# A state-space input product: one stacked float32r product in place of a plain float32 one

## The chip, the core and the metric

The kernel runs on one core of a Trainium2 chip. The metric is the device time of one execution in microseconds (us). Five engines work in it, each through its own instructions in a fixed order: TensorE (PE: matrix products; its weight loads are listed as PEld), VectorE (DVE), ScalarE (ACT), GpSimd (POOL) and SyncE (SP). SP and POOL also issue the transfers (DMA) between memory and the on-chip buffers.

## What is computed

Two blocks of a network over 256 tokens of 2048 features: a feed-forward part, then a mixer of a state-space half and an attention half, another feed-forward part, and a second block. The change lies in the state-space half. Each group of 16 channels drives 64 complex states; the input to the states is a small product per group:

```python
def s5_mixer(u, log_dt, a_re, a_im, b_re, b_im, c_re, c_im, d, w_glu, b_glu):
    ...
    bu_re = jnp.einsum('bsgh,gph->sbgp', u32, bb_re)
    bu_im = jnp.einsum('bsgh,gph->sbgp', u32, bb_im)
    ...
    _, _, s_re, s_im = lax.associative_scan(_ssm_combine, (a_re_t, a_im_t, bu_re, bu_im), axis=0)
    y = (jnp.einsum('sbgp,ghp->bsgh', s_re, c_re.astype(f32))
         - jnp.einsum('sbgp,ghp->bsgh', s_im, c_im.astype(f32))
         + d.astype(f32) * u32)
```

## The kernel before

**Big products.** All large products go through `gemm` (line 220). Weights are loaded by SP in pieces `raw` (three buffers), ACT rounds half a piece (a unit) to a first float32r part `whi` (line 100), and DVE makes the rest `wlo` (line 110), up to three units ahead of their use. Activations are held in two parts too (`xTh`, `xTl`). A product then is three: hi hi, hi lo, lo hi (lines 240 to 242 with 512 columns, "form B"; lines 248 to 250 with 256 columns, "form T"), accumulated in PSUM tiles `acc`. One unit is 12 products of form B or 24 of form T.

**Side work and its order.** After each unit `tick` (line 194) runs deferred closures and steps side tasks: Python generators that emit a few instructions and then yield the DVE time that they have used, or a pair of that and a number of ticks to wait. `K.finish(task)` (line 212) emits all that is left of a task at that place, with no product in between. Nothing reorders what was emitted: each engine takes its instructions in that order.

**The early chain.** `block1` spawns one chain of side tasks, `early`, under the first feed-forward part: constants, `mod_vectors`, `ctx_norm`, `ssm_prep` (tables of the states), and `mod_rows` (line 518). The last one sums, for two rows and in four halves of 16 pieces of `w_mod`, `macc += mraw * cs` on DVE (line 543: 32 instructions a half, `mraw` loaded by SP through line 534), and then turns each sum by transposes on PE (`mp`, line 553: 16 a half) and reduces them on DVE (line 554). Behind the feed-forward part stands `K.finish(*early)`, and then the input product of the mixer, form T, whose first 1024 columns become `uT` (line 955).

**The state-space part.** `ssm_states` (line 632) is a side task in 16 steps `jp` of two 32-channel groups `j`. `fetch` loads ahead, by POOL's queue, the input matrix `sB`, the output matrix `sC` and the rotation table `rot`. For each group, PE makes `bu` (line 673): two plain float32 products with 32 rows of contraction and 256 columns, straight from `uT`. DVE rotates (`ssw`, `sst`, lines 675 to 681), scans (686) and rotates back (688 to 692), POOL adds (694, 695), and PE multiplies by `sC` (`sy`, line 656). It runs under the mixer's input product and the context's products. `mid` (`m4`) is a pool of ten 4 KB buffers that most of these tiles share.

Of the kernel before, what the change touches and what calls it, by code (L numbers as in the profile page):

```python
# [16 lines left out]
P = 128  # L17
# [6 lines left out]
class Nul:  # L24
    """Stands for every object of the dry pass, which only lists the weight pieces in their order."""
# [17 lines left out]
class Parts(tuple):  # L43
    """The two parts of a k-tile; two: those of it and the next one together."""


class Stream:
    """Weights come in pieces [128, nk, w] (one load each) and are split exactly into two float32r
    parts, half a piece at a time, ahead of the products."""
# [40 lines left out]
    def round(self, upto):  # L90
        """The first parts of the units."""
        K = self.K
        while self.nh < min(upto, len(self.units)):
            p, u, nu, w = self.units[self.nh]
            if u == 0:
                self.load(p + self.RAW)
                self.raw.pop(p - 2, None)
            raw = self.raw[p][:, u * w:u * w + nu * w]
            hi = K.wpool.tile([P, 1024], F32R, tag="whi", name="whi", bufs=self.HI + 1)
            K.nc.scalar.activation(hi[:, :nu * w], raw, AF.Copy)  # L100
            self.parts[self.nh] = hi, raw, nu * w
            self.nh += 1

    def split(self, upto):
        """The second parts of the units."""
# [18 lines left out]
class Core:  # L124
# [22 lines left out]
    # -- tiles -----------------------------------------------------------------  # L147
    def b8(self, name, shape=(P, 2048), dt=F32):
        """A tile of the 8 KB class."""
        return self.big.tile(list(shape), dt, tag="b8", name=name)  # L150

    def m4(self, name, shape=(P, 1024), dt=F32):
        """A tile of the 4 KB class."""
        return self.mid.tile(list(shape), dt, tag="m4", name=name)

    def t1(self, name, shape=(P, 256), dt=F32):
        """A tile of the 1 KB class."""
        return self.sm.tile(list(shape), dt, tag="t1", name=name, bufs=6)

    def t2(self, name, shape=(P, 514), dt=F32):  # L160
        """A tile of the 2 KB class."""
# [11 lines left out]
    # -- order -----------------------------------------------------------------  # L173
# [8 lines left out]
    def step(self, task):  # L182
        """One step of a side task; it yields the vector engine's load of it or (load, ticks to wait)."""
# [21 lines left out]
    def flush(self):  # L205
        """Everything that was deferred, now."""
# [12 lines left out]
    # -- products --------------------------------------------------------------  # L219
    def gemm(self, form, name, kts, n0, w, xT, evac, early=False):  # L220
        """form 'B': tokens on partitions, acc[:, tt, :w]. form 'T': columns on partitions,
        acc[:, nt // 2, (nt % 2) * 256:][:256]. xT[kt]: the two parts [128, 256] of x transposed.
        early: the first pieces are small."""
# [31 lines left out]
    def new_xT(self, n=16, name="xT"):  # L255
        """Room for n k-tiles of a transposed operand in both parts."""
# [9 lines left out]
    def to_xT(self, src, kts, xT, gain=None):  # L266
        """Transposes src(kt, tt) [128 tokens, 128 features] into xT, times gain(kt) [128, 1]."""
# [24 lines left out]
    def rsqrt(self, x, shape, name):  # L292
        """1 / sqrt(x) of a small tile, to full precision: a first guess from the bits, then Newton."""
# [17 lines left out]
class Norm:  # L311
    """Mean square of a token's features, gathered chunk by chunk; then 1 / rms."""
# [21 lines left out]
def ffn(K, w, xT, rstd, h, finished, before_last=None):  # L334
    """h += 0.5 * (silu(x gate) * (x up)) down; finished(n) when the columns n of h are final."""
# [64 lines left out]
def exp_exact(K, x, shape, name, out):  # L400
    """exp of a small tile to float32's precision."""
# [15 lines left out]
def ssm_prep(K):  # L417
    """The state's decay, its angle in turns, and c times (lambda - 1) / a; then the rotation tables."""
# [64 lines left out]
    # cos and -sin of the angle at every token, two states' tiles at a time  # L483
# [22 lines left out]

def mod_vectors(K):
# [10 lines left out]
def mod_rows(K, rows, thirds):  # L518
    """silu(c) w_mod + b_mod of rows: shift and 1 + scale with features on partitions, gate as a row."""
# [48 lines left out]
def layer_stats(K, x, name):  # L568
    """mean and 1 / std of [128, 2048] rows."""
# [25 lines left out]
def token_row(K, r, name):  # L595
    """A value per token (tokens on partitions, [128, 2]) as a row on all partitions [128, 256]."""
# [9 lines left out]
class TokenSquares:  # L606
    """Sum over features of squares, for values with features on partitions."""
# [24 lines left out]
def ssm_states(K, uT):  # L632
    """y, before the gelu and then after it, in the place of u, channels on partitions; its parts to yT."""
    nc, v, a = K.nc, K.nc.vector, K.a
    B, C, E = {}, {}, {}

    def fetch(jp):
        if jp >= 16:
            return
        if jp % 2 == 0:  # L640
            kt = jp // 2
            B[kt] = K.t1("sB", (P, 2, 128))
            nc.gpsimd.dma_start(B[kt][:], a["s_b"][kt])
            C[kt] = K.t1("sC", (P, 2, 4, 32))
            for i in range(2):
                nc.gpsimd.dma_start(C[kt][:, i], K.cfold[i, :, 4 * kt:4 * kt + 4, :])
        E[jp] = K.m4("rot", (P, 2, 2, 256))
# [16 lines left out]
    for jp in range(16):  # L664
        kt, half = divmod(jp, 2)
# [3 lines left out]
        for j in range(2):  # L669
            b = K.ps("bu", (P, 2, 256))  # L670
            q = 32 * (2 * half + j)
            for ri in range(2):
                nc.tensor.matmul(b[:, ri], B[kt][q:q + 32, ri], uT[q:q + 32, kt, :], start=ri == 0, stop=True,  # L673
                                 skip_group_check=True)
# [19 lines left out]
        nc.gpsimd.tensor_add(t[:, 0], t[:, 0], w[:, 0])  # L694
        nc.gpsimd.tensor_sub(w[:, 1], w[:, 1], t[:, 1])
        del E[jp]
        last = jp, t[:, 0], w[:, 1]
# [6 lines left out]
def ssm_gelu(K, uT, yT):  # L704
    """gelu in place, and its two parts."""
# [10 lines left out]
def attend1(K, qT, kT, vt, mix, sq):  # L716
    """Heads by pairs; the three dilated branches as one softmax: mask = 8 log(times a key is seen)."""
# [65 lines left out]
def conv(K, acc, kts, y, scale):  # L783
    """Three taps along the tokens and silu, features on partitions: y[:, n] from the columns' tile kts[n]."""
# [17 lines left out]
def ctx_columns(K, xT):  # L802
    """The columns of block 2's input product that the context feeds: k, v, gates, k and v of the attention."""
# [40 lines left out]
def ctx_values(K, xT):  # L844
    """The context's values of the attention: work for the time in which block 2's input is normed."""
# [11 lines left out]
def ctx_again(K, xT):  # L857
    """The context's operand from memory into both parts."""
# [14 lines left out]
def next_norm(K, h, gain, name, xT, R, spill=None):  # L873
    """What follows each final chunk of h: its part of the rms and its transposes, into xT."""
# [36 lines left out]
def block1(K):  # L911
# [24 lines left out]
    early = [K.spawn(chain(constants1(K), mod_vectors(K), ctx_norm(K), ssm_prep(K), mod_rows(K, (0, 1), (0, 1))))]  # L936

    # ---- ffn 1, and the next norm as its columns become final
# [6 lines left out]
    # ---- the input product: u first, then q, k, v  # L945
# [12 lines left out]

    for dst, n0 in ((uT, 3072), (qT, 0), (kT, 1024)):
        for i in range(2):  # L960
            K.gemm("T", "w_in", kx, n0 + 512 * i, 512, xT2, keepT(dst, i))
# [39 lines left out]
    # ---- the context's part of block 2's input product, under which the mixers run  # L1001
# [56 lines left out]
    # ---- the ssm's half of the output product, then ffn 2  # L1058
# [10 lines left out]
def affine(K, p, kt, row, dst):  # L1069
    """x (1 + scale) + shift of two k-tiles [128, 512], features on partitions, into both parts."""  # L1070
# [14 lines left out]
def log_sigmoid(K, x, sh, out):  # L1085
    """min(x, 0) - log1p(exp(-|x|)); the log by the odd series of (y - 1) / (y + 1). A generator."""
# [17 lines left out]
def gate_rows(K, raw, m0):  # L1104
    """From the gates' columns [128, 2, 32]: b (sums of log f), a = i - b and M = max(m0, running max of a),
    heads on partitions, [8, dir, 256]; dir 1 runs back in time. A generator; leaves K.gr = (b, a, M)."""
# [35 lines left out]
def rows_to_cols(K, rows, name):  # L1142
    """[8, dir, 256] to tokens on partitions [128, t, dir, 8]."""
# [11 lines left out]
def ctx_post(K):  # L1155
    """The context's final state of both mLSTMs, and its keys for the attention."""
# [66 lines left out]
def head_rms(K, x, name):  # L1223
    """1 / rms of 4 heads of 128: x [128, 2, 512] to [128, 8] (t, head)."""
# [9 lines left out]
def rope(K, x, cs, out):  # L1234
    """out = x * cos + turned x * sin, with the norm's weights in the tables cs = (cos, sin) [128, 2, 128]."""
# [639 lines left out]
```

## Time and profile before

| | us |
|---|---|
| median of three runs | 3209.63 |
| lowest, highest | 3209.04, 3209.82 |
| profiled execution, span | 3209.2 |
| PE busy | 3182.3 (99%) |
| DVE busy | 2249.9 (70%) |
| ACT busy | 1484.6 (46%) |
| POOL busy | 264.6 (8%) |

The profile is one execution. A busy share is an average over stages; what a stage costs is read from the order in time. A float32 product of `bu` shows as two records, a float32r one as one. "x8" in a row of the timeline is eight records merged, with the time from the start of the first to the end of the last; since products are pipelined, what one costs on PE is the distance from its start to the next one's.

### The profile page before, as it was taken

Reading aid. Unit: us, or ns where it says so; the run is one execution under the profiler, and the core shown is the slowest. Engines: PE = TensorE matmul, PEld = TensorE weight load, DVE = VectorE, ACT = ScalarE, POOL = GpSimd, SP = SyncE. Lnnn points to the kernel's source line nnn. Section 1 sums busy time; section 2 is a strip of 40 time slices with the busy share of each in tenths; the row PEclk is TensorE's granted clock in tenths of the full one; section 3 lists DMA queues with packets and bytes.
Section 4 is the critical chain, followed back from the end, with each engine's and each line's share of the span. In section 5 each row is a group of like instructions: output and inputs, shape, how many; then the busy total and the mean of one; then the engine's idle time right before and its main releaser. Section 6 shows DMA issues by size and latency. Waiting matters only on the chain.

```text
span 3209.2 us, 41935 instructions
## 1 busy us (share of the span) xinstructions
PE 3182.3 (99%) x16088; PEld 2686.5 (84%) x16088; DVE 2249.9 (70%) x3224; ACT 1484.6 (46%) x1939; POOL 264.6 (8%) x411
## 2 busy tenths in 40 slices
PE   8999999999999999999999999999999999999998
PEld 7888888889978788888888888889988888888887
DVE  6768798786987886764766546767656875445667
ACT  5574444444346445544444444545544444444442
POOL 1000000000231221001000000000001110000001
PEclk9999999999999999999999999999999999999999
DMA  7678677775564555556766556554445555655653
GB/s 266 242 266 289 237 269 263 264 257 201 191 223 159 178 210 203 198 192 207 293 248 241 204 187 220 219 197 171 144 161 175 181 184 205 225 194 186 231 215 132
DMA packets 117146, 684.32 MB, mean 213 GB/s; under 512 B 15612, under 2 KB 15900, under 8 KB 52172
## 3 DMA queue, kind: packets, MB, share of 16 engines
q1 hardware_dynamic: 95616, 610.90, 53.2%
q0 software_dynamic: 21328, 70.74, 6.4%
q8 instruction: 126, 2.06, 0.3%
q14 instruction: 76, 0.61, 0.1%
HBM read 646.41 MB, written 35.18 MB: 212 GB/s over the span
## 4 chain that ended last, share of the span: by engine, by line
PE 97%; DVE 1%; DMA 1%; issue 0%; POOL 0%; ACT 0%; DVEq 0%; SPq 0%; POOLq 0%; ACTq 0%
PE acc L240 27%; PE acc L242 26%; PE acc L241 26%; PE acc L248 3%; PE acc L249 3%; PE acc L250 3%; PE tr L275 1%; PE mN L1429 1%; PE o2p L1343 1%; PE bu L673 1%; PE s L1321 1%; PE sy L656 0%; PE pt L1333 0%; PE ap L726 0%; PE cp L1208 0%
## 5 line engine op out<-in xcount | busy, mean ns | idle before, releaser
L110 DVE TENSOR_TENSOR wlo<-raw,whi 128x1024 fp32r<-128x1024 f32 (+3 forms) x1088 | 1300.2, 1205 | 508.7 <-PE acc L241 411.1
L100 ACT ACTIVATE whi<-raw 128x1024 fp32r<-128x1024 f32 (+3 forms) x1088 | 1115.5, 1031 | 1151.1 <-PE acc L242 920.2
L240 PE MATMUL acc<-whi,xTh 128*128 128x512 f32 (+1 forms) x1472 | 570.9, 388 | 1.9 <-ACT whi L100 1.7
L241 PE MATMUL acc<-wlo,xTh 128*128 128x512 f32 (+1 forms) x1472 | 567.8, 386 | 1.0 <-DVE wlo L110 1.0
L242 PE MATMUL acc<-whi,xTl 128*128 128x512 f32 (+1 forms) x1472 | 567.6, 386 | 0.3 <-DVE xTl L290 0.3
L240 PE MATMUL acc<-whi,uT2h 128*128 128x512 f32 (+2 forms) x992 | 387.5, 391 | 0.0
L242 PE MATMUL acc<-whi,uT2l 128*128 128x512 f32 (+2 forms) x992 | 380.9, 384 | 0.0
L241 PE MATMUL acc<-wlo,uT2h 128*128 128x512 f32 (+2 forms) x992 | 380.3, 383 | 0.0
L240 PEld LDWEIGHTS acc<-whi,xTh 128*128 128x128 f32 x1472 | 277.1, 188 | 58.2 <-issue 2.6
L241 PEld LDWEIGHTS acc<-wlo,xTh 128*128 128x128 f32 x1472 | 277.1, 188 | 53.0 <-DVE wlo L110 2.0
L242 PEld LDWEIGHTS acc<-whi,xTl 128*128 128x128 f32 x1472 | 276.9, 188 | 53.1 <-DVE xTl L290 0.6
L240 PE MATMUL acc<-whi,gTh 128*128 128x512 f32 x688 | 269.5, 392 | 0.5 <-DVE h L375 0.5
L242 PE MATMUL acc<-whi,gTl 128*128 128x512 f32 x688 | 268.3, 390 | 0.0
L241 PE MATMUL acc<-wlo,gTh 128*128 128x512 f32 x688 | 268.1, 390 | 0.0
L240 PEld LDWEIGHTS acc<-whi,uT2h 128*128 128x128 f32 x992 | 186.6, 188 | 37.2 <-issue 2.5
L242 PEld LDWEIGHTS acc<-whi,uT2l 128*128 128x128 f32 x992 | 186.5, 188 | 36.8
L241 PEld LDWEIGHTS acc<-wlo,uT2h 128*128 128x128 f32 x992 | 186.7, 188 | 35.2
L543 DVE SCALAR_TENSOR_TENSOR macc<-mraw,cs,macc 128x1024 f32<-128x1024 f32 x160 | 204.6, 1279 | 3.6 <-DMA mraw<-w_mod 3.6
L240 PE MATMUL acc<-whi,wTh 128*128 128x512 f32 (+1 forms) x416 | 157.2, 378 | 0.0
L241 PE MATMUL acc<-wlo,wTh 128*128 128x512 f32 (+1 forms) x416 | 155.5, 374 | 1.2 <-DVE wlo L110 1.2
L242 PE MATMUL acc<-whi,wTl 128*128 128x512 f32 (+1 forms) x416 | 155.4, 374 | 0.0
L240 PEld LDWEIGHTS acc<-whi,gTh 128*128 128x128 f32 x688 | 129.3, 188 | 27.0 <-ACT whi L100 0.9
(538 smaller groups left out, 4393.1 us busy)
## 6 DMA issues: line engine op xcount, KB each, us to landing
raw<-w_w_in SPq DMA_DIRECT2D x192, 1024.0 KB, 4.9
raw<-w_ffn_w_gate SPq DMA_DIRECT2D x80, 1024.0 KB, 4.9
raw<-w_ffn_w_up SPq DMA_DIRECT2D x80, 1024.0 KB, 4.9
raw<-w_ffn_w_down SPq DMA_DIRECT2D x80, 1024.0 KB, 4.9
mraw<-w_mod SPq DMA_DIRECT2D x96, 512.0 KB, 6.2
raw<-w_w_out SPq DMA_DIRECT2D x28, 1024.0 KB, 4.8
rot<-rot POOLq DMA_DIRECT2D x32, 512.0 KB, 5.0
raw<-w_w_branch_b SPq DMA_DIRECT2D x16, 1024.0 KB, 4.9
```

Source lines behind the costliest of these rows:

```text
L100: K.nc.scalar.activation(hi[:, :nu * w], raw, AF.Copy)
L110: K.nc.vector.tensor_sub(lo[:, :n], raw, hi[:, :n].bitcast(F32))
L240: nc.tensor.matmul(o, xh[:, ts], wh, start=first, stop=False)
L241: nc.tensor.matmul(o, xh[:, ts], wl, start=False, stop=False)
L242: nc.tensor.matmul(o, xl[:, ts], wh, start=False, stop=last)
L248: nc.tensor.matmul(o, wh[:, ns], xh, start=first and n % 2 == 0, stop=False, **sk)
L249: nc.tensor.matmul(o, wh[:, ns], xl, start=False, stop=False, **sk)
L250: nc.tensor.matmul(o, wl[:, ns], xh, start=False, stop=last, **sk)
L275: nc.tensor.transpose(p[:, o:o + 128], src(kt, t), self.ident[:])
L543: v.scalar_tensor_tensor(accs[row][:], w[:], K.cs[:, row, kt:kt + 1], accs[row][:], op0=OP.mult, op1=OP.add)
L673: nc.tensor.matmul(b[:, ri], B[kt][q:q + 32, ri], uT[q:q + 32, kt, :], start=ri == 0, stop=True, skip_group_check=True)
L1321: nc.tensor.matmul(p[:], l[:, t * 128:t * 128 + 128], kk[:, r], start=i == 0, stop=i == 2)
```

## The change

Both operands of `bu` come in two float32r parts, stacked along the contraction: `u` as hi, hi, lo (the first 32 rows, the next 32, the last 32), the input matrix as hi, lo, hi. So one product with 96 rows replaces the float32 one with 32. The parts are made beforehand and go through memory:

- a new side task `ssm_inputs_prep` stands in the early chain ahead of `ssm_prep`: eight times it loads a 96x1024 piece of the (host-side tripled) matrix, rounds it on ACT, subtracts on DVE and stores it to `bst`; its yields are `0, 3`, `0, 1` and `1200`;
- after each half of `uT`, ACT and DVE make `uh` and `ul`, and POOL's queue stores both to `ust`;
- `fetch` loads, in place of one `sB` for two steps, for each step three pieces of `ust` and one of `bst` into a tile `us`;
- POOL's addition writes to `w[:, 0]` and no longer to `t[:, 0]`.

```diff
+def ssm_inputs_prep(K):
+    nc, v = K.nc, K.nc.vector
+    K.bst = K.dram.tile([96, 8192], F32R, name="bst")
+    for c in range(8):
+        cs = slice(c * 1024, c * 1024 + 1024)
+        x, z = K.m4("bx", (96, 1024)), K.m4("bz", (96, 1024), F32R)
+        nc.gpsimd.dma_start(x[:], K.a["s_b"][:, cs])
+        yield 0, 3
+        nc.scalar.activation(z[:], x[:], AF.Copy)
+        yield 0, 1
+        v.tensor_sub(z[32:64], x[32:64], z[32:64].bitcast(F32))
+        nc.gpsimd.dma_start(K.bst[:, cs], z[:])
+        yield 1200
...
-            B[kt] = K.t1("sB", (P, 2, 128))
-            nc.gpsimd.dma_start(B[kt][:], a["s_b"][kt])
...
+        U[jp] = K.m4("us", (96, 2, 512), F32R)
+        for i in range(3):
+            nc.gpsimd.dma_start(U[jp][32 * i:32 * i + 32, 0].rearrange("r (j t) -> r j t", j=2),
+                                K.ust[i // 2, jp // 2, jp % 2].rearrange("j r t -> r j t"))
+        nc.gpsimd.dma_start(U[jp][:, 1], K.bst[:, jp * 512:jp * 512 + 512])
...
-            q = 32 * (2 * half + j)
             for ri in range(2):
-                nc.tensor.matmul(b[:, ri], B[kt][q:q + 32, ri], uT[q:q + 32, kt, :], start=ri == 0, stop=True,
-                                 skip_group_check=True)
+                o = (2 * j + ri) * 128
+                nc.tensor.matmul(b[:, ri], U[jp][:, 1, o:o + 128], U[jp][:, 0, j * 256:j * 256 + 256], start=ri == 0,
+                                 stop=True, skip_group_check=True)
...
-        nc.gpsimd.tensor_add(t[:, 0], t[:, 0], w[:, 0])
+        nc.gpsimd.tensor_add(w[:, 0], t[:, 0], w[:, 0])
...
-        last = jp, t[:, 0], w[:, 1]
+        last = jp, w[:, 0], w[:, 1]
...
-    early = [K.spawn(chain(constants1(K), mod_vectors(K), ctx_norm(K), ssm_prep(K), mod_rows(K, (0, 1), (0, 1))))]
+    early = [K.spawn(chain(constants1(K), mod_vectors(K), ctx_norm(K), ssm_inputs_prep(K), ssm_prep(K), mod_rows(K, (0, 1), (0, 1))))]
...
+        def parts():
+            ks = slice(4 * i, 4 * i + 4)
+            hi, lo = (K.m4(n, (P, 4, 256), F32R) for n in ("uh", "ul"))
+            nc.scalar.activation(hi[:], uT[:, ks], AF.Copy)
+            v.tensor_sub(lo[:], uT[:, ks], hi[:].bitcast(F32))
+            for x, z in enumerate((hi, lo)):
+                nc.gpsimd.dma_start(K.ust[x, ks].rearrange("k a j r t -> (a j r) k t"), z[:])
...
-            K.gemm("T", "w_in", kx, n0 + 512 * i, 512, xT2, keepT(dst, i))
+            K.gemm("T", "w_in", kx, n0 + 512 * i, 512, xT2, keep_u(i) if dst is uT else keepT(dst, i))
```

The order of the instructions shows what this moves. Lines of the changed kernel differ from those of the kernel before: the sums are line 559 there (543 before), the transposes 569 (553), the reductions 570 (554).

PE, where the first feed-forward part (products with `gT`) ends and the mixer's input product (with `xT`) begins; `mp` are the transposes of `mod_rows`. Before:

```order
L240 MATMUL acc<-whi,gTh 128x512
L241 MATMUL acc<-wlo,gTh 128x512
L242 MATMUL acc<-whi,gTl 128x512
L248 MATMUL acc<-xTh,whi 128x256
L249 MATMUL acc<-xTl,whi 128x256
L250 MATMUL acc<-xTh,wlo 128x256
```

After:

```order
L241 MATMUL acc<-wlo,gTh 128x512
L242 MATMUL acc<-whi,gTl 128x512
L569 MATMUL mp<-ident,macc 128x128 x16
L248 MATMUL acc<-xTh,whi 128x256
L249 MATMUL acc<-xTl,whi 128x256
L250 MATMUL acc<-xTh,wlo 128x256
```

The last 16 transposes of the early chain, which before stood in two groups of eight, five and four units (60 and 48 products) ahead of this border, now stand on it.

DVE at the same border: `h` is the last sum of the feed-forward part, `n2` the norm behind it, `macc` the sums of `mod_rows`. Before, from the last transposes of `h` on:

```order
L290 SCALAR_TENSOR_TENSOR xTl<-tr,gains,xTh 128x256 x4
L110 TENSOR_TENSOR wlo<-raw,whi 128x1024 x2
L375 SCALAR_TENSOR_TENSOR h_83<-acc,h_83 128x512
L375 SCALAR_TENSOR_TENSOR h_84<-acc,h_84 128x512
L325 TENSOR_REDUCE n2ms<-n2ss 128x2
```

After:

```order
L290 SCALAR_TENSOR_TENSOR xTl<-tr,gains,xTh 128x256 x4
L559 SCALAR_TENSOR_TENSOR macc<-mraw,cs,macc 128x1024
L110 TENSOR_TENSOR wlo<-raw,whi 128x1024
L559 SCALAR_TENSOR_TENSOR macc<-mraw,cs,macc 128x1024
L110 TENSOR_TENSOR wlo<-raw,whi 128x1024
L559 SCALAR_TENSOR_TENSOR macc<-mraw,cs,macc 128x1024
L375 SCALAR_TENSOR_TENSOR h_83<-acc,h_83 128x512
L375 SCALAR_TENSOR_TENSOR h_84<-acc,h_84 128x512
L325 TENSOR_REDUCE n2ms<-n2ss 128x2
```

and, behind the norm's small steps,

```order
L301 TENSOR_TENSOR n2rt<-n2ry 128x2
L302 SCALAR_TENSOR_TENSOR n2rt<-n2rt,n2ms 128x2
L303 SCALAR_TENSOR_TENSOR n2ry<-n2rt,n2ry 128x2
L559 SCALAR_TENSOR_TENSOR macc<-mraw,cs,macc 128x1024 x29
L570 TENSOR_REDUCE modT<-mp 128x4 x2
L573 TENSOR_SCALAR modT<-modT 128x8
```

Three sums of the last half of `mod_rows` now stand ahead of the last `h`, and the other 29 in one piece behind the norm; before, all 32 were spread over earlier units.

POOL, from the last spill of `h` to the first step of `ssm_states`. Before:

```order
L882 DMA hspill<-h_84 128x512
L643 DMA sB<-s_b 128x256
L646 DMA sC<-cfold 128x128 x2
L648 DMA rot<-rot 128x1024 x2
L694 ISA
```

After:

```order
L901 DMA hspill<-h_84 128x512
L989 DMA ust<-uh 128x4x256
L989 DMA ust<-ul 128x4x256
L989 DMA ust<-uh 128x4x256
L989 DMA ust<-ul 128x4x256
L660 DMA sC<-cfold 128x128 x2
L664 DMA us<-ust 32x2x256 x3
L666 DMA us<-bst 96x512
L668 DMA rot<-rot 128x1024
```

The loads of the first step now stand behind the stores of `ust`, which wait for `uT`. Everywhere else the side work on PE stands between the same products as before.

## Rows read from the trace of the kernel before

**Rows 1.** Page, part 1: engine, busy us (share of span), instructions

```profile
PE 3182.3 (99%) x16088; PEld 2686.5 (84%) x16088; DVE 2249.9 (70%) x3224; ACT 1484.6 (46%) x1939; POOL 264.6 (8%) x411
```

**Rows 2.** Page, chain that ended last, shares by engine

```profile
PE 97%; DVE 1%; DMA 1%; issue 0%; POOL 0%; ACT 0%; DVEq 0%; SPq 0%; POOLq 0%; ACTq 0%
```

**Rows 3.** Timeline of PE, first bu: start, us, operation, [idle before <- releaser]

```profile
794.31 0.28 PE L249 MATMUL acc<-xTl,whi 128*128 128x256 f32 x1
794.43 0.28 PE L250 MATMUL acc<-xTh,wlo 128*128 128x256 f32 x1
794.64 1.14 PE L673 MATMUL bu<-uT,sB 32*128 32x256 f32 x8
795.71 0.38 PE L248 MATMUL acc<-xTh,whi 128*128 128x256 f32 x1
795.93 0.28 PE L249 MATMUL acc<-xTl,whi 128*128 128x256 f32 x1
```

**Rows 4.** Timeline of PE, a bu of one group alone

```profile
1137.79 1.13 PE L673 MATMUL bu<-uT,sB 32*128 32x256 f32 x4
1138.85 0.40 PE L240 MATMUL acc<-whi,cTh 128*128 128x288 f32 x1
```

**Rows 5.** Chain in order of time (start, us, what), middle of the stage

```profile
947.29 2.26 POOL ssw L695
```

**Rows 6.** Windows: length, then busy PE, PEld, DVE, ACT, POOL; PEclk, DMA, GB/s

```profile
840.00:880.00 40.00, 40.00 (x317) 36.97 (x316) 36.40 (x50) 12.10 (x12) 10.61 (x9) 1.00 0.52 182
...
1150.00:1160.00 10.00, 9.39 (x65) 7.41 (x64) 9.94 (x16) 2.88 (x6) 4.52 (x4) 1.00 0.45 142
```

**Rows 7.** Timeline of PE at the end of the first feed-forward part

```profile
738.55 0.39 PE L242 MATMUL acc<-whi,gTl 128*128 128x512 f32 x1
738.78 0.28 PE L248 MATMUL acc<-xTh,whi 128*128 128x256 f32 x1
```

**Rows 8.** Timeline of DVE at the same place

```profile
735.52 2.35 DVE L110 TENSOR_TENSOR wlo<-raw,whi 128x1024 fp32r<-128x1024 f32 x2
738.98 1.29 DVE L375 SCALAR_TENSOR_TENSOR h<-acc,h 128x512 f32<-128x512 f32 x2 [1.11 <-PE acc L242]
...
743.52 2.36 DVE L110 TENSOR_TENSOR wlo<-raw,whi 128x1024 fp32r<-128x1024 f32 x2
```

**Rows 9.** Timeline of DVE, a sum of mod_rows between two splits

```profile
350.17 1.22 DVE L110 TENSOR_TENSOR wlo<-raw,whi 128x1024 fp32r<-128x1024 f32 x1
351.31 1.28 DVE L543 SCALAR_TENSOR_TENSOR macc<-mraw,cs,macc 128x1024 f32<-128x1024 f32 x1
352.50 1.22 DVE L110 TENSOR_TENSOR wlo<-raw,whi 128x1024 fp32r<-128x1024 f32 x1
```

**Rows 10.** Chain in order of time: the last transposes of mod_rows

```profile
722.63 0.87 PE mp L553 x8
726.25 0.87 PE mp L553 x8
```

**Rows 11.** Timeline of PE behind its waits at 1167 to 1171

```profile
1173.03 0.63 PE L240 MATMUL acc<-whi,mixAh 128*128 128x512 f32 x1
1173.46 0.63 PE L241 MATMUL acc<-wlo,mixAh 128*128 128x512 f32 x1
...
1177.87 0.39 PE L240 MATMUL acc<-whi,mixAh 128*128 128x512 f32 x1
1178.10 0.39 PE L241 MATMUL acc<-wlo,mixAh 128*128 128x512 f32 x1
```

**Rows 12.** Windows, the same place (columns as in rows 6)

```profile
1170.00:1175.00 5.00, 4.82 (x16) 3.74 (x17) 4.59 (x14) 1.06 (x1) 1.17 (x3) 0.57 0.67 228
```

**Rows 13.** Timelines of DVE and of ACT, the second half of uT

```profile
786.11 1.29 DVE L955 TENSOR_TENSOR uT<-acc,rb 128x512 f32<-128x512 f32 x2 [1.60 <-PE acc L250]
...
785.99 1.06 ACT L100 ACTIVATE whi<-raw 128x1024 fp32r<-128x1024 f32 x1 [1.82 <-PE acc L249]
```

**Rows 14.** Instructions of tile rot: its transfers, issue to landing

```profile
DMA to landing us min/median/max: 2.9/5.0/8.1
```

**Rows 15.** Timelines of POOL and PE: last table's load, and the bu it serves

```profile
1140.87 0.56 POOL L648 DMA_DIRECT2D rot<-rot  x1
...
1151.04 1.12 PE L673 MATMUL bu<-uT,sB 32*128 32x256 f32 x4
```

More of the change, by code (lines that the diff above doesn't have):

```diff
@@ L43 @@
 class Parts(tuple):
+    pass
 class Stream:
@@ L634, in ssm_states @@
     nc, v, a = K.nc, K.nc.vector, K.a
-    B, C, E = {}, {}, {}
+    U, C, E = {}, {}, {}
     def fetch(jp):
@@ L664, in ssm_states @@
     for jp in range(16):
-        kt, half = divmod(jp, 2)
         fetch(jp + 1)
@@ L693, in ssm_states @@
         yield 1200
-        nc.gpsimd.tensor_add(t[:, 0], t[:, 0], w[:, 0])
+        nc.gpsimd.tensor_add(w[:, 0], t[:, 0], w[:, 0])
         nc.gpsimd.tensor_sub(w[:, 1], w[:, 1], t[:, 1])
-        del E[jp]
-        last = jp, t[:, 0], w[:, 1]
+        del E[jp], U[jp]
+        last = jp, w[:, 0], w[:, 1]
         yield 100
@@ L957, in keepT, with keep_u, both @@
         return ev
+    K.ust = K.dram.tile([2, 8, 2, 2, 32, 256], F32R, name="ust")
+    def keep_u(i):
+        ev = keepT(uT, i)
+        def parts():
[5 more added lines that the diff above has]
+                nc.gpsimd.dma_start(K.ust[x, ks].rearrange("k a j r t -> (a j r) k t"), z[:])
+        def both(acc):
+            ev(acc)
+            parts()
+        return both
     for dst, n0 in ((uT, 3072), (qT, 0), (kT, 1024)):
         for i in range(2):
-            K.gemm("T", "w_in", kx, n0 + 512 * i, 512, xT2, keepT(dst, i))
+            K.gemm("T", "w_in", kx, n0 + 512 * i, 512, xT2, keep_u(i) if dst is uT else keepT(dst, i))
         if dst is uT:
@@ L1823, in small @@
         for g in range(2): z[:,:,g,:,q,g,:]=Bm[:,:,g].transpose(0,1,3,2)
-    a["s_b"]=z.reshape(8,128,2,128)
+    z=z.reshape(16,2,32,256).transpose(2,0,1,3).reshape(32,8192)
+    a["s_b"]=np.ascontiguousarray(np.concatenate([z]*3))
     a["c_x"]=cols(I["c_2"][0],16); a["c_ctx"]=cols(I["c_ctx_2"],16)
```

## The prediction

> **What bounds the kernel now.** First the page's busy shares: PE is busy 99% of the span [rows 1]. Then the chain that ended last: 97% of it lies on PE [rows 2], so PE's own instruction stream is the clock of this kernel, and whatever makes PE stand still is paid in full. The other engines count where PE waits for them. Third, the timeline of PE where the change works: products of 256 columns follow each other at 0.12 us, and a group of `bu` stands among them [rows 3, 4]. Last, since the diff adds steps to a chain of side tasks, the end of the first feed-forward part, where that chain is forced to its end: there PE goes from the last product of one part to the first of the next without a pause (738.55 to 738.78) [rows 7].
>
> **The product itself (gain).** A group alone holds PE from 1137.79 to 1138.85, 1.06 us [rows 4]; two groups of one step that stand side by side take 1.07 together (794.64 to 795.71) [rows 3]. Around it come 0.09 before (0.21 where neighbours stand 0.12 apart) and 0.10 behind (0.22 for 0.12) [rows 3]: 1.25 and 1.26. Afterwards a group is two float32r products of 256 columns, in the shape of those beside it. No row shows one with 96 rows; the nearest are the 128-row ones at 0.12 [rows 3], so 0.24 a group and 0.48 a pair. From above, were each of the two to cost what the old product did, 0.53, a group would save 0.19 (the borders) and a pair nothing. I take 0.24 since type and column count are those of the neighbours: 1.01 saved by a group alone, 0.78 by a pair. In PE's order five of the 16 steps have their groups side by side, eleven apart (22 groups).
>
> The Trainium skill speaks against the change here: "TensorEngine Tiling (Array Packing)", section "Tiling Modes", says that 32-row tiles work in parallel, which a 96-row product gives up. The pair's 1.07 against 1.06 for one [rows 3, 4] agrees. If all 16 steps stood in pairs, the rule would leave 16 x 0.78 = 12.5 us of gain and not 25; but eleven have other products between their groups. The same section says that a change of tiling mode drains the engine, which would explain the 0.09 and 0.10; by it they go with the new shape, and if they stay, the gain is 24 x 0.19 = 4.6 us less.
>
> Not all of this is worth its price. The last step (two groups) lies where DVE is busy 9.94 of 10 us [rows 6], and one pair where the chain runs through POOL and DVE [rows 5]: nothing. That leaves 20 x 1.01 + 4 x 0.78 = 23.3 us. DVE is also full elsewhere: 36.4 of 40 us in an early part of the stage [rows 6], where PE would save about 3 of its 40 and DVE has 3.6 to give. So some becomes waiting for DVE; I take 19. Bounds: 24, and 10 (a group at 0.65, midway between its two prices, saves 0.6 and a pair nothing: 20 x 0.6 = 12, less 2 to DVE).
>
> **The early chain (loss).** `ssm_inputs_prep` has little work: per piece one ACT and one DVE instruction of about 1 us, hidden under the feed-forward part, where PE doesn't wait. But it waits by ticks: 3 and 1, and one more after `1200`, so 5 for each of eight pieces, 40 ticks. Everything behind it in the chain is 40 units later: the first group of `mp` stands 480 products later in PE's order, which is 40 x 12. The chain had only about four units to spare before the border: its last transposes ran at 726.25 [rows 10], its border is 738.78 [rows 7]. So the remaining half of `mod_rows` is emitted by `K.finish(*early)` at one place: 29 sums on DVE, then 16 transposes on PE, ahead of the first product of the mixer. PE takes its instructions in order, so it stands at the first transposes until DVE has done 28 sums, and has nothing else, though three units are split.
>
> How long? Before, DVE is done with the split behind `xTl` at 737.87, starts the last `h` at 738.98 after 1.11 us of idle time, and is through the norm at 743.52 [rows 8]. Three sums now stand ahead of `h`. A sum holds DVE for 1.19 us (351.31 to 352.50) [rows 9], so 3.6 less the idle 1.1: 2.5 late. The 29 start at 743.5 + 2.5 = 746.0. They need 28 x 1.19 + 1.28 = 34.6 us and end at 780.6. Each pair needs a 512 KB `mraw`, one per 2.4 us; ten buffers let SP run ahead, so I take DVE as the bound. Then eight transposes, 0.87 us [rows 10]: the first product starts at about 781.5 in place of 738.78, 42.7 later. The 16 transposes moved here free 1.74 us plus borders, say 1.9, earlier. Net **+41**. Bounds: 38 (the three sums fit into idle time) and 45 (1.28 us a sum, transposes at half clock).
>
> After a wait PE is slow: behind the waits near 1170 its granted clock is 0.57 of full [rows 12] and products stand 0.43 apart (1173.03 to 1173.46) until some 4 us later it is 0.23 (1177.87 to 1178.10) [rows 11]; 0.43 and 0.23 are the levels of 1.2 and 2.4 GHz. Thirteen products at 0.20 more are 2.6 us. After 40 us of waiting the same comes once: **+3** (2.6 to 4).
>
> **The first step's operands (loss).** Before, the first `bu` needed only `uT` and an early load. Now: `uT` at 787.4, `uh` on ACT 1.06 [rows 13], `ul` on DVE about 1.2 as a split [rows 9], so 789.7; then POOL issues the store of `ul`, two `sC`, three `us` and one `bst`, 0.55 each [rows 15], the last from 793.0. A transfer of this queue lands 5.0 us after its issue (2.9 to 8.1) [rows 14]: 798.0, where `bu` stood at 794.64 [rows 3]. PE waits behind it: **+3** (1 to 6.5, or 0 if POOL has issued ahead). Behind the new wait on DVE for `uh` stand splits, covered by three units, about 8 us. Later steps load a whole step ahead: the last starts at 1140.87 for a `bu` at 1151.04 [rows 15]; five issues and 5.0 us end at 1148.7. Zero, with 2 us to spare. POOL's addition into `w` only frees a buffer sooner.
>
> **The sum.** -19 + 41 + 3 + 3 = +28 on the profiled span of 3209.2: 3237.2. The median of the runs, 3209.63, is 0.4 above that span: **3237.6 us**, 0.9% slower.
>
> **Rivals.** (1) *The new product costs what the old did*, or DVE swallows the gain: the loss stays, 3209.6 + 47 = 3257. For it: no row with 96 rows, DVE's fill. Against: neighbours at 0.12. (2) *Operands late at every step*: POOL's queue does five issues a step in place of 1.5, and at 8.1 us landing the last would come at 1151.8, behind its `bu`. 2 us in each of 16 steps would be 32 more: 3270. Against: earlier steps have twice the distance. (3) *Faster: the 29 sums do not stop PE.* The place is the border at 738.8. It decides where the wait costs 19 - 3 - 3 = 13 us net in place of 41: with 7.2 us from the border to the first sum, 0.9 for transposes and 1.9 freed, (13 - 7.2 - 0.9 + 1.9) / 29 = 0.23 us a sum. Were the sums quicker than that, or the transposes passed by the ready products, the time would be below before; without the loss, 3209.6 - 19 + 3 = 3194. For it: DVE is only 70% busy [rows 1], and three units are ready. Against: 1.19 us a sum [rows 9], PE's order. (4) *The early chain is late but ends in time*, and gain and first load nearly cancel what is left: within 0.2%.
>
> **How the numbers follow.** Forecast 0.74; (1) 0.10; (2) 0.09; (3) 0.04; (4) 0.03. A measurement of this kernel can tell about 0.2% (6.4 us) from no change. Slower 0.93, same 0.03, faster 0.04. Range: low 38 + 2.6 + 0 - 24 = +17, 3226; high 45 + 4 + 6.5 - 10 = +45.5, 3255, and to 3257 with rival (1).
>
> **What would show it.** In the profile after: PE idle some 41 us in one piece near 737, released by a sum of `mod_rows` (`macc`); 29 sums back to back on DVE at about 1.2 us; a granted clock of half behind it. `bu` with 64 records of 0.12 us each, not 128. One wait of a few us at the first `bu`, released by a transfer. The stretch from the first `bu` to the last `sy` some 19 us shorter. I am wrong if PE's long wait is missing or under 13 us, if `bu` is not under 0.3 us a product, or if many steps wait for `us`.

## The result and the profile after

The changed kernel takes 3242.53 us (median; 3241.62 to 3246.57) against 3209.73 of the kernel before, measured beside it: a ratio of 1.0101, interval 1.0088 to 1.0115. Forecast were 3237.6 and slower. The profiled execution has a span of 3239.6 us in 3241.62; before, 3209.2.

Page of the changed kernel, part 1 (columns as in [rows 1]):

```profile
PE 3160.1 (98%) x16024; PEld 2677.0 (83%) x16024; DVE 2261.1 (70%) x3234; ACT 1495.5 (46%) x1949; POOL 308.3 (10%) x487
```

PE has 64 instructions fewer and is busy 22.2 us less, yet the span is 30.4 longer: PE stands still for longer. Where, the waits of PE tell (line waited, what released it: us in total, times, longest). The first five of the changed kernel:

```profile
PE mp L569 <- issue: 40.6, 1, 40.6
PE bu L692 <- DMA us<-bst: 9.0, 1, 9.0
PE co L1762 <- DVE oco L1759: 6.8, 1, 6.8
PE tr L275 <- DMA h<-x: 6.0, 2, 5.8
PE sy L676 <- POOL ssw L714: 3.8, 3, 1.5
```

and of the kernel before:

```profile
PE co L1725 <- DVE oco L1722: 6.8, 1, 6.8
PE tr L275 <- DMA h<-x: 5.6, 2, 5.4
PE sy L656 <- POOL ssw L695: 2.9, 3, 1.6
```

The two at the top are new. The first lies at the border of the feed-forward part and the mixer. Timeline of PE there, the answer to [rows 7]:

```profile
737.35 0.39 PE L242 MATMUL acc<-whi,gTl 128*128 128x512 f32 x1
778.35 3.65 PE L569 MATMUL mp<-ident,macc 128*128 128x128 f32 x16 [40.61 <-issue]
781.65 0.56 PE L248 MATMUL acc<-xTh,whi 128*128 128x256 f32 x1
782.01 0.41 PE L249 MATMUL acc<-xTl,whi 128*128 128x256 f32 x1
782.22 0.41 PE L250 MATMUL acc<-xTh,wlo 128*128 128x256 f32 x1
782.43 0.36 PE L248 MATMUL acc<-xTh,whi 128*128 128x256 f32 x1
782.64 0.28 PE L249 MATMUL acc<-xTl,whi 128*128 128x256 f32 x1
```

"issue" names no releaser, but the timeline of DVE does, the answer to [rows 8]:

```profile
738.96 1.27 DVE L559 SCALAR_TENSOR_TENSOR macc<-mraw,cs,macc 128x1024 f32<-128x1024 f32 x1
740.16 1.28 DVE L375 SCALAR_TENSOR_TENSOR h<-acc,h 128x512 f32<-128x512 f32 x2
...
744.69 34.76 DVE L559 SCALAR_TENSOR_TENSOR macc<-mraw,cs,macc 128x1024 f32<-128x1024 f32 x29
779.47 0.69 DVE L570 TENSOR_REDUCE modT<-mp 128x4 f32<-128x512 f32 x1
```

29 sums stand in one piece, 1.2 us each. The transposes start at 778.35, when 28 of them are through. All 16 take 3.30 us (before, eight took 0.87 [rows 10]), since the granted clock there is half, 0.50:

```profile
778.00:782.00 4.00, 3.65 (x17) 3.68 (x18) 3.65 (x6) 0.00 (x0) 0.00 (x0) 0.50 0.00 0
```

(columns as in [rows 6]). The mixer's first product starts at 781.65 in place of 738.78: 42.9 us later.

The second new wait is the first step's. Timelines of PE and of POOL, the answer to [rows 3]:

```profile
847.09 1.23 PE L692 MATMUL bu<-us 96*128 96x256 f32 x4 [8.99 <-DMA us<-bst]
848.11 0.41 PE L248 MATMUL acc<-xTh,whi 128*128 128x256 f32 x1
...
833.43 0.74 POOL L989 DMA_DIRECT2D ust<-ul  x1 [0.51 <-DVE ul L987]
834.16 1.12 POOL L660 DMA_DIRECT2D sC<-cfold  x2
835.26 1.69 POOL L664 DMA_DIRECT2D us<-ust  x3
836.90 0.58 POOL L666 DMA_DIRECT2D us<-bst  x1
```

The load of `bst` needs nothing of the stores ahead of it, and is issued at 836.90; PE gets its data at 847.1. The instructions of `us` by stretch, first step (835.2 to 836.95) and all steps behind the second (860 to 1200), issue to landing, and the 16 loads of `rot` in the kernel before (740 to 1200):

```profile
DMA to landing us min/median/max: 10.1/10.6/11.0
...
DMA to landing us min/median/max: 2.1/4.1/8.3
...
DMA to landing us min/median/max: 3.5/4.2/6.7
```

Elsewhere the product does what was hoped. A group alone and a pair, in the timeline of PE:

```profile
866.71 0.28 PE L250 MATMUL acc<-xTh,wlo 128*128 128x256 f32 x1
866.83 0.40 PE L692 MATMUL bu<-us 96*128 96x256 f32 x2
867.06 0.28 PE L248 MATMUL acc<-xTh,whi 128*128 128x256 f32 x1
...
882.63 0.64 PE L692 MATMUL bu<-us 96*128 96x256 f32 x4
883.10 0.28 PE L248 MATMUL acc<-xTh,whi 128*128 128x256 f32 x1
```

0.23 and 0.47 us, with no gap beyond the neighbours' 0.12. From the first `bu` to the start of the last `sy` the stage takes 356.1 us (847.1 to 1203.2); before, 375.8 (794.6 to 1170.4).

| stretch | before, us | after, us | difference |
|---|---|---|---|
| to the mixer's first product | 738.8 | 781.65 | +42.9 |
| to the first bu | 55.9 | 65.4 | +9.6 |
| first bu to last sy | 375.8 | 356.1 | -19.7 |
| behind it | 2038.8 | 2036.4 | -2.4 |
| span | 3209.2 | 3239.6 | +30.4 |

The 2.4 us behind the stage are no finding: in the other kernels of this study that leave it untouched the same stretch took 2035.9 to 2041.0 us.

### The profile page after: what moved, and what is told of

Read it like the earlier page. It is cut to its first block, busy times and chain, and to the rows that moved or that the text cites. A ratio compares the mean times of both kernels' runs of the same rounds, so it can differ in the third digit from the quotient of the medians.

```text
span 3239.6 us, 41982 instructions
## 1 busy us (share of the span) xinstructions
PE 3160.1 (98%) x16024; PEld 2677.0 (83%) x16024; DVE 2261.1 (70%) x3234; ACT 1495.5 (46%) x1949; POOL 308.3 (10%) x487
## 4 chain that ended last, share of the span: by engine, by line
PE 65%; DVE 2%; issue 1%; POOL 0%; DMA 0%; ACT 0%; DVEq 0%; POOLq 0%; ACTq 0%
PE acc L240 18%; PE acc L241 18%; PE acc L242 18%; PE acc L248 2%; PE acc L249 2%; PE acc L250 2%; PE mN L1466 1%; PE o2p L1380 1%; PE s L1358 1%; PE tr L275 1%; DVE wlo L110 0%; PE pt L1370 0%; PE ap L745 0%; PE cp L1245 0%; PE sy L676 0%
```

## The experiments

Ten kernels were run, each beside the kernel before (3210.8 to 3211.3 us there, 1.7 us of it around the span). Most undo one part; "stage" is the time from the first `bu` to the start of the last `sy`.

**Is it the delay? `ticks40`: the kernel before with empty ticks.** Nothing of the change but its 40 ticks.

```diff
+def empty_ticks(n):
+    for _ in range(n):
+        yield 0, 1
...
-    early = [K.spawn(chain(constants1(K), mod_vectors(K), ctx_norm(K), ssm_prep(K), mod_rows(K, (0, 1), (0, 1))))]
+    early = [K.spawn(chain(constants1(K), mod_vectors(K), ctx_norm(K), empty_ticks(40), ssm_prep(K), mod_rows(K, (0, 1), (0, 1))))]
```

> The kernel before with 40 empty ticks in the early chain, ahead of ssm_prep, and nothing else: no parts, no new product. My theory (being 40 units late is enough): 29 sums stand behind the norm on DVE, PE waits some 40.6 us for them and does 16 transposes at half clock; the border is 42.9 us longer: span 3209.2 + 42.9 = 3252, time about 3252.5. Rival (the delay is harmless without the parts' own DVE work and transfers): under 3215.

Measured: 3254.88 us, ratio 1.0137 (1.0122 to 1.0152), span 3252.5; the mixer's first product at 781.5. Waiting without any work costs what the change lost at the border, within 0.2 us.

**Fixed part and price per sum. `ticks12`: the same with 12 ticks.**

> The kernel before with 12 empty ticks in the early chain instead of 40: only 2 sums stand behind the norm on DVE, but the same 16 transposes stand at the border. My theory (the wait has a fixed part, the norm that DVE does first, 738.5 to 744.6, plus 1.19 us a sum, plus transposes at half clock): PE waits about 7.5 to 9 us and then does 16 transposes in up to 3.3 us, the border costs 11 us more than in the kernel before, time about 3221. Rival (the price is the sums' alone, 42.9 us for 29): 2 sums cost 3 us, time about 3213.

Measured: 3223.85 us, ratio 1.0040 (1.0025 to 1.0055). Timeline of PE at the border:

```profile
739.86 0.39 PE L242 MATMUL acc<-whi,gTl 128*128 128x512 f32 x1
749.34 3.65 PE L559 MATMUL mp<-ident,macc 128*128 128x128 f32 x16 [9.09 <-issue]
752.64 0.56 PE L248 MATMUL acc<-xTh,whi 128*128 128x256 f32 x1
```

That is 12.9 us over the kernel before, 2 us more than expected. From the last product to the first are 12.8 us (739.86 to 752.64) where 0.23 stood: a wait of 9.1 us for the norm that stands ahead of the sums on DVE and for the two sums, and 3.3 us of transposes at half clock. In `ticks40` PE waits 40.6 us, so the 27 sums more add (40.6 - 9.1) / 27 = 1.17 us each. The rival (3 us) is out: some 10 us of the border's price are there before the sums count.

**Undoing the delay. `prep_side`: the preparation as a side task of its own.**

```diff
-    early = [K.spawn(chain(constants1(K), mod_vectors(K), ctx_norm(K), ssm_inputs_prep(K), ssm_prep(K), mod_rows(K, (0, 1), (0, 1))))]
+    early = [K.spawn(chain(constants1(K), mod_vectors(K), ctx_norm(K), ssm_prep(K), mod_rows(K, (0, 1), (0, 1))))]
+    early.append(K.spawn(ssm_inputs_prep(K)))
```

> The changed kernel with ssm_inputs_prep taken out of the early chain and spawned as a side task of its own; the work is the same, and mod_rows stands between the same products as in the kernel before. My theory (the place in the chain costs the time): the wait of 40.6 us at the border of the feed-forward part and the mixer goes, the 16 transposes at half clock (3.3 us) go back to 2 x 0.87 us, so the border costs 42.9 us less: span 3239.6 - 42.9 = 3196.7, time about 3198.7 (2.0 us lie around the span). The 9 us wait at the first bu stays. Rival (it is the added work of the parts, its transfers and its DVE time, that makes the chain late): the last transposes run late all the same, PE waits 20 us or more at the border, time above 3220.

Measured: 3214.21 us, ratio 1.0008 (0.9999 to 1.0018), profiled span 3213.9. The long wait is gone, but 15 us of the expected gain are missing. Timelines of PE, of DVE and of POOL of this kernel:

```profile
62.61 0.80 PE L241 MATMUL acc<-wlo,xTh 128*128 128x512 f32 x1 [9.12 <-DVE wlo L110]
...
56.33 2.47 DVE L591 BATCH_NORM_STATS2 cnst<-ctx 128x6 f32<-128x512 f32 x4 [7.93 <-DMA ctx<-ctx]
...
32.27 0.52 POOL L519 DMA_DIRECT2D bst<-bz  x1 [29.68 <-ACT junk L320]
...
43.90 0.54 POOL L602 DMA_DIRECT2D ctx<-ctx  x1
```

Here the preparation began at once, so its first store stood in POOL's queue ahead of the constants and of the context's load, and POOL waited for it until 32.27; it issued `ctx` only at 43.90 (at 10.06 in the kernel before), DVE waited for it in order, and the splits behind it came late for PE. The mixer's first product came at 750.6, 11.8 of the 15 us. A new loss, of this remedy's own making.

**The same, started later. `prep_lag`.**

```diff
-    early.append(K.spawn(ssm_inputs_prep(K)))
+    early.append(K.spawn(chain(iter([(0, 36)]), ssm_inputs_prep(K))))
```

> Only the first remedy: ssm_inputs_prep as its own side task, started 36 ticks late; the first step's loads as in the changed kernel. My theory (prep_side fell short because POOL's queue held back the load of ctx): no wait for wlo near 60 us, the mixer's first product at 739 as in the kernel before, the wait of 9 us at the first bu still there: span 3197 to 3201, time 3199 to 3203. Rival (the shortfall of prep_side lies elsewhere too): 3206 or more.

Measured: 3204.50 us, ratio 0.9979 (0.9970 to 0.9988), span of the profiled run 3200.5. The first product stands at 740.6, the wait of 8.9 us at the first `bu` is still there, the stage takes 356.0. The median is 1.5 us above the expectation's range, the profiled span in it. The border alone decided between slower and faster.

**The first step. `first_ahead`: two steps' loads ahead of the second half's stores.**

```diff
     fetch(0)
-    yield 0, 2
+    fetch(1)
+    yield 0, 10
...
-        fetch(jp + 1)
+        if jp:
+            fetch(jp + 1)
...
-        if dst is uT:
-            ssm = K.spawn(ssm_states(K, uT))
+            if dst is uT and i == 0:
+                ssm = K.spawn(ssm_states(K, uT))
```

> The changed kernel with ssm_states spawned after the first half of uT, so that the loads for the steps 0 and 1 (which need only that half) are issued ahead of the stores of the second half; the first bu stays at its place (lag 10 for 2). My theory (the first step's table waits in POOL's queue behind the two stores of the second half): the wait of 9.0 us at the first bu goes, and with it the half clock behind it (bu 1.02 for 0.48 and 12 products 0.09 us longer, 1.6 us): span 3239.6 - 10.6 = 3229, time about 3231. Rival (the queue stays late, and the wait moves to step 1 or 2): 3236 to 3243, with a wait for us at a later bu.

Measured: 3234.13 us, ratio 1.0073 (1.0058 to 1.0088), profiled span 3234.3. The first `bu` follows the product ahead of it at 0.12 us:

```profile
839.89 0.28 PE L250 MATMUL acc<-xTh,wlo 128*128 128x256 f32 x1
840.01 0.64 PE L694 MATMUL bu<-us 96*128 96x256 f32 x4
840.49 0.28 PE L248 MATMUL acc<-xTh,whi 128*128 128x256 f32 x1
```

From the mixer's first product to it are 56.6 us, 8.8 less than in the changed kernel; the stage takes 354.3, 1.8 less, since nothing runs at half clock behind it. That is the expected 10.6. The time fell by 8.4 only: the profiled run is 1.7 us late already at the border and 3.6 behind the last `sy`, where neither kernel differs. No later `bu` waits. The loads of the first step still stand behind two stores of 512 KB, those of the first half, and the DMA engines are as full as they were (a busy share of 1.11 from 815 to 829; in the changed kernel 1.09 from 838 to 847). Instructions of `us` from 815 to 821.2:

```profile
DMA to landing us min/median/max: 4.9/6.7/8.3
```

What this run gives them is time: the last is issued at 820.74, 19 us ahead of the first `bu`. Whether the place behind the stores or the load on the DMA engines makes such transfers slow, no run here separates.

**The product's type. `plain_hi`: a float32 product of the first 32 rows.** Hi lo and lo hi are left out.

```diff
-                nc.tensor.matmul(b[:, ri], U[jp][:, 1, o:o + 128], U[jp][:, 0, j * 256:j * 256 + 256], start=ri == 0,
-                                 stop=True, skip_group_check=True)
+                nc.tensor.matmul(b[:, ri], U[jp][0:32, 1, o:o + 128].bitcast(F32),
+                                 U[jp][0:32, 0, j * 256:j * 256 + 256].bitcast(F32), start=ri == 0, stop=True,
+                                 skip_group_check=True)
```

> The changed kernel, with all its parts, stores and loads, but bu as a plain float32 product of the first 32 rows of us (the products hi lo and lo hi are left out). My theory (the product's type is the gain): a group costs 1.06 us and its borders again in place of 0.24, the stretch from the first bu to the last sy is 19 to 20 us longer, span 3259, time about 3261. Rival (the shorter stretch comes from elsewhere, such as POOL's addition that frees a buffer sooner, or fewer waits): within 5 us of the changed kernel, 3243 to 3248.

Measured: 3270.70 us, ratio 1.0187 (1.0172 to 1.0203). The stage takes 381.8, 25.7 more than after and 6 more than before. So the product is the gain: with all other parts of the change the stage is no shorter than before. Of the 6 us some 4.3 have a place, since a pair takes 1.92 us where before it took 1.07 [rows 3], five times; the rest is about what half clock behind the first wait cost in the changed kernel too (1.8). Timeline of PE:

```profile
888.21 1.99 PE L692 MATMUL bu<-us 32*128 32x256 f32 x8
890.13 0.39 PE L248 MATMUL acc<-xTh,whi 128*128 128x256 f32 x1
```

**`plain_rows`: the second group on other rows.** The same with `U[jp][32 * j:32 * j + 32]` for `U[jp][0:32]`, so that the two groups of a pair lie on different rows (the second then multiplies other parts than the first).

> As plain_hi, a plain float32 product with 32 rows, but the second group of a step reads rows 32 to 63 of us and not the first 32 (parts of the product are left out, as there). My theory (two 32-row products on different rows run at the same time, on the same rows one after the other): the pairs of groups take 1.07 us again and not 1.92, five of them, so the stretch from the first bu to the last sy is 4.3 us shorter than in plain_hi, 377.5 in place of 381.8; time about 3266. Rival (the 1.92 comes from something else in the tile us): within 1 us of plain_hi's stretch.

Measured: 3268.46 us, ratio 1.0176 (1.0161 to 1.0192); the stage takes 378.3, 3.5 less than in `plain_hi`. The pair is back at 1.07:

```profile
888.43 1.14 PE L692 MATMUL bu<-us 32*128 32x256 f32 x8
889.50 0.38 PE L248 MATMUL acc<-xTh,whi 128*128 128x256 f32 x1
```

So here 32-row products on different rows ran at the same time, on the same rows one after the other.

**The number of rows. `hi_only`: float32r, 32 rows.** Only hi hi.

```diff
-                nc.tensor.matmul(b[:, ri], U[jp][:, 1, o:o + 128], U[jp][:, 0, j * 256:j * 256 + 256], start=ri == 0,
-                                 stop=True, skip_group_check=True)
+                nc.tensor.matmul(b[:, ri], U[jp][0:32, 1, o:o + 128], U[jp][0:32, 0, j * 256:j * 256 + 256],
+                                 start=ri == 0, stop=True, skip_group_check=True)
```

> The changed kernel with float32r products of the first 32 rows of us alone (hi hi; the other two parts are left out). My theory (type and columns set the price, not rows): a group stays at 0.24 us and a pair at 0.48, the stretch from the first bu to the last sy stays at 356 us, time 3242 (3240 to 3246). Rival 1 (the Trainium skill, TensorEngine Tiling (Array Packing), section Tiling Modes: a change of tiling mode drains the engine): the 0.09 us ahead of a group and the 0.10 behind it are there again, 24 groups x 0.19 = 4.6 us more, stretch 360.7. Rival 2 (fewer rows, less time): a group under 0.2 us and the stretch shorter.

Measured: 3252.94 us, ratio 1.0130 (1.0116 to 1.0143): 10 us slower than with 96 rows. The stage takes 365.4 in place of 356.1. Timeline of PE, a group alone:

```profile
866.45 0.28 PE L250 MATMUL acc<-xTh,wlo 128*128 128x256 f32 x1
866.66 0.50 PE L692 MATMUL bu<-us 32*128 32x256 f32 x2
867.09 0.39 PE L248 MATMUL acc<-xTh,whi 128*128 128x256 f32 x1
867.31 0.28 PE L249 MATMUL acc<-xTl,whi 128*128 128x256 f32 x1
```

0.21 us ahead, 0.43 within, 0.22 behind: 0.86 where 96 rows take 0.12 + 0.23 + 0.12. That is 0.39 a visit; 27 visits (22 groups alone and five pairs) make 10.5, and the stage grew by 9.3, of which some 0.8 is half clock that lasts longer behind the first wait (848.7 to 854.9, where it was 847.1 to 850.9). A pair takes 0.67 within (886.30 to 886.97), so its second group adds 0.24, the neighbours' price: what is extra is paid once a visit, not by the product. My theory that only type and columns set the price fell; so did its opposite, that fewer rows take less time. The 9.3 are twice the 4.6 us of rival 1: I had counted the gaps around a group, and not the 0.2 inside. The Trainium skill, "TensorEngine Tiling (Array Packing)", section "Tiling Modes", says that a change of tiling mode drains the engine. The trace agrees with it, by a price of 0.39 us a visit; that the drain is the cause, no run shows by itself.

**Another remedy. `fin_late`: the sums spread under the mixer.** `K.finish(*early)` stands behind the fifth 512 columns of the mixer's input product and not at the border.

```diff
-    K.finish(*early)
     K.share = 1600.0
...
             K.gemm("T", "w_in", kx, n0 + 512 * i, 512, xT2, keep_u(i) if dst is uT else keepT(dst, i))
+            if dst is kT and i == 0:
+                K.finish(*early)
```

> The changed kernel with K.finish(*early) moved from the border to behind the fifth 512 columns of the mixer's input product: the 29 sums are no longer forced at one place but spread as side work over the next 20 units of form T, and ssm_states starts 8 units later. My theory (the wait at the border is order, but the sums still need DVE's time, and here it is scarce): the wait of 40.6 us goes (42.9 us with the half clock); a unit holds PE for 2.88 us and DVE for 2.34 us of splits plus 1.45 sums of 1.19 us, 4.07; 20 units lack 24 us, of which three units made ahead cover about 8: PE waits some 16 us in small pieces for wlo. Time 3242.5 - 42.9 + 16 = 3216 (3211 to 3224). Rival (DVE has room, all is hidden): 3199.

Measured: 3210.14 us, ratio 0.9999 (0.9989 to 1.0009), 1 us below the range I gave, by misses of both signs. The long wait is gone. From the mixer's first product to the first `bu` are 76.3 us (739.8 to 816.1), 20.5 more than in `both` below; 11.5 of them are four units more (not eight), so the sums cost some 9 us here, and not 16: PE waits 4.8 us for `wlo` in five pieces, and the granted clock is 0.82 from 770 to 780. The first `bu` no longer waits, for its loads have four units more to land; this I had not taken off. What I had not added is the stage: it takes 367.1 us, 12.8 more than in `both`, with a granted clock of 0.91 from 935 to 955 and 0.83 from 1155 to 1175. PE waits 11.3 us there for what POOL makes for `sy`, against 5.1 in the changed kernel:

```profile
PE sy L676 <- POOL ssw L714: 6.5, 5, 1.6
PE sy L676 <- POOL ssw L713: 4.8, 4, 2.5
```

Why the later steps come late, no run separates. Windows of this kernel (columns as in [rows 6]):

```profile
750.00:760.00 10.00, 9.60 (x79) 9.24 (x78) 10.00 (x12) 2.63 (x3) 0.00 (x0) 1.00 0.66 256
...
770.00:780.00 10.00, 7.15 (x49) 6.95 (x48) 8.87 (x9) 4.84 (x5) 1.53 (x2) 0.82 0.88 284
```

DVE is full where the sums went, and this remedy returns less than `prep_lag`, which leaves them where DVE has room.

**Both remedies. `both`: `prep_lag` with `first_ahead`.** The diffs of these two together.

> Two remedies at once: ssm_inputs_prep as a side task of its own that starts 36 ticks late (behind the context's norm), and the loads of the steps 0 and 1 ahead of the stores of the second half, as in first_ahead. My theory: the border's 42.9 us and the first bu's 10.6 us go, and, unlike in prep_side, nothing delays the load of ctx near 50 us: span 3239.6 - 53.5 = 3186; the stretch behind the last sy was up to 4 us longer in the runs on this chip, so 3186 to 3190, time 3188 to 3192, ratio 0.993 to 0.994. Rival (the parts' work costs DVE time somewhere however it is placed): 3198 or more, with PE waits for wlo in the first feed-forward part.

Measured: 3190.12 us, ratio 0.9938 (0.9925 to 0.9950): faster than either kernel, by 0.6% than the one before. The first two waits of PE:

```profile
PE co L1765 <- DVE oco L1762: 6.8, 1, 6.8
PE tr L275 <- DMA h<-x: 6.1, 2, 5.9
```

They are those of the kernel before. The stage takes 354.3 us (795.8 to 1150.1).

## Why the prediction was right

It named the two places and the signs; its total was 4.9 us low, and that it came so near is in part luck, since errors of single steps cancelled. By its own steps:

- **The border (+41 and +3).** Right in mechanism, place and size, shown by `ticks40`. The three sums ahead delayed `h` as assumed: it starts 2.8 us after the last product (740.16 against 737.35), where it started 0.4 after it (738.98 [rows 8], 738.55 [rows 7]), so 2.4 late where I had 2.5. The first product came 2.2 us behind the last sum (779.45) and not 0.87, for the transposes run at half clock. That is also where most of the clock's price was paid: 1.6 us in the transposes (3.30 against 2 x 0.87), and behind them only four slow products (781.65 to 782.64, 0.99 us where 0.48 is usual), not thirteen as in [rows 11]. From last product to first product the border grew by 44.1, and the last one came 1.2 earlier, where I had freed 1.9. That gain is not shown: in the four experiments whose PE stream is the same up to there, the last product came at 738.3 to 739.2. Together 42.9 + 0.5, against 44.
- **The product (-19).** The stage is 19.7 us shorter. The borders went with the rows as assumed: 0.23 us a group, 0.47 a pair. But the near hit hides an error: 1.8 us of half clock behind the first wait are in it. Undisturbed, in `both` and `first_ahead`, the stage is 21.5 us shorter, close to the 23.3 of PE's own sum. About 2 were lost to waits, not the 4 that I took off for DVE: PE stands still 6.3 us in the stage of `both`, 3.8 in that of the kernel before, most of it for POOL's additions.
- **The first step's operands (+3).** This step failed in size: 9.0 us of waiting, and 1.8 of half clock behind it (the stage's 356.1 against 354.3), beyond my bound of 6.5. The issues were right: the last one came 6.1 us after `uT` (830.8 to 836.90), where I had 5.6. The landing was not: 10.1 to 11.0 us, where I took the 5.0 of [rows 14]. Half of the transfers in those rows are stores of the tables, made under the first feed-forward part; the 16 loads alone landed in 3.5 to 6.7 us, with the DMA engines at a busy share of 0.55 (740 to 1145). In the changed kernel two stores of 512 KB stood directly ahead, in a queue that I had listed but not priced, and the DMA engines were full; which of the two made the loads slow stays open.
- **Later steps (0).** Right: no other `bu` waits, so rival 2 is out, with 4.1 us from issue to landing in the middle.
- **The sum.** Forecast were -19 + 41 + 3 + 3 = 28; measured 43.4 - 21.5 + 9.0 + 1.8 - 2.4 = 30.3 of the 30.4 in span. The 7.8 us too little at the first step were mostly made up by the product (2.5) and by the stretch behind the stage (2.4, no finding, so luck). The other 2.5 of the 4.9 lie outside the span: 2.0 us around it in the changed kernel, where I carried over 0.4, and 0.9 by which the profiled run, the fastest of four, was below the median. In the later runs 1.7 lie around the span of the kernel before too, so my 0.4, the median of three runs less one profiled span, was no measure of it.
- **The rivals.** (1) is out by the stage, (3) by the border: a sum cost 1.2 us, far from 0.23, and PE did not pass its transposes. (4) did not happen here, but `prep_lag` shows what it describes: with the chain in time the kernel is 0.2% faster than before, and the rest of the change together is a gain.

## What to carry to other kernels

Where side work ends at a forced point, a chain's ticks are its price even where they wait for nothing: before putting a step into it, count the units between its end and that point, and give the step a lane of its own, started where no queue ahead of it matters. When operands begin to travel through memory, price the first load with the stores ahead of it and the DMA engines as full as they will be, not by a median from elsewhere, or issue it early. And a small product among full-height ones can gain by more rows: here 0.39 us a visit went with the 32 rows.

## What the runs showed of the hardware

- A 256-column float32r product took 0.12 us with 96 rows as with 128. With 32 rows it cost 0.39 us more a visit (0.86 against 0.47, gaps included) among products of 128 rows.
- A float32 product of that shape: a pair of groups on the same rows took 1.92 us, a group 1.06, so one product is (1.92 - 1.06) / 2 = 0.43 and 0.20 is fixed. Of the 1.01 us that a group saved, 2 x 0.31 is the type and about 0.39 the rows.
- Two 32-row groups on different rows took 1.07 us together, on the same rows 1.92.
- After 9 us of waiting as after 40 us, PE's granted clock was 0.50 (1.2 GHz), and products stood at their usual distance again some 4 us after it resumed in the changed kernel (778.35 to 782.6; 847.1 to 850.9), 3.3 in `prep_lag` and 6.6 in `plain_rows`.
